# Pairing the float32 products between the projection groups of a hybrid attention and mLSTM layer

## The chip, the cores and the metric

The kernel runs on one core of a Trainium2 chip. The metric is the device time in microseconds (us) of one execution; of several executions the median is given.

## What is computed

One layer over 256 tokens of width 1024, in float32. A normalised and modulated input `h` is multiplied by a wide matrix `w_in`, and the result is cut into the inputs of two mixers. The first mixer is causal softmax attention with eight heads, the second an mLSTM with four. Both outputs are gated, normalised, projected, added and projected again:

```python
h = _rmsnorm(x, norm_w) * (1 + scale) + shift
(qa, ka, va, za, qm, km, vm, zm, om, ig, fg, ga, gm) = jnp.split(h @ w_in, SPLIT_IDX, axis=-1)
ya = merge(_moba_attention(qa, ka, heads(va, ATT_HEADS), rel_bias))
ya = (ya * jax.nn.silu(za)) @ w_att_proj
qk = jax.nn.silu(_causal_dwconv(jnp.concatenate([qm, km], axis=-1), conv_w, conv_b))
...
hm = _mlstm_chunkwise(...)
hm = jax.nn.sigmoid(heads(om, ML_HEADS)) * hm
hm = _rmsnorm(hm, ml_norm_w)
ym = (merge(hm) * jax.nn.silu(zm)) @ w_ml_proj
y = jax.nn.sigmoid(ga) * ya + jax.nn.sigmoid(gm) * ym
return x + gate * (y @ w_out)
```

With 256 tokens the attention has a single block, and the kernel computes the mLSTM in its parallel form: decayed scores times values.

## The kernel before

**Phase one** (until about 58 us) loads `x`, the modulation weights and the first columns of `w_in`, normalises, and makes `hTh` and `hTl`: the modulated input, transposed, split into a part that the type float32r holds and the rest. Nothing of it is changed.

**The projection groups.** The rest of all projections is cut into 25 chunks of 512 output columns: ka, va (two halves), za, qm, km, att, zm, vm, om, ga, gm, ml and out, each later one in two halves. A chunk has four groups, so there are 100 groups, counted by `g`; a group covers 256 rows of the contraction. For each group the weights are split into `wh` (ScalarE, L423) and `wl` (VectorE, L427, in a few groups GpSimd), and TensorE multiplies in three products: high by high, low by high, high by low. All of these are float32r. In chunks of kind `ws` (za, qm, km, att, ga, gm, ml) the weights are the stationary operand; there a group is 24 products of 256 columns (L964, L966, L967), from the loops over two `kk`, four `i` and three products. In chunks of kind `tok` (ka, va, zm, vm, om) it is 12 products of 512 columns (L957 to L959).

**The ring.** `wh` and `wl` have five buffers each. At the start of group g the program issues the split of group g + 4, so a split that is late by less than about three groups holds nobody up.

**The mixers' own work** stands between the groups. `at(step, fn, args)` puts a function into a list, and at each group g the functions of that list run before the group's products are issued. Since all engines take their instructions in the program's order, the step number sets where on each engine the function's instructions stand. A number is written as `done(name, half)`, the first group after that chunk, plus an offset. The functions that matter here multiply plain float32, not float32r:

- `att_av(h0)` (L609): probabilities times values for two heads. TensorE L617 and L619; then VectorE L623 and ScalarE L624 and GpSimd L625, which make `yah` and `yal`, the moving operand of chunk att.
- `ml_scores(h)` (L714): scores of one mLSTM head, four products at L720, two of 128 and two of 256 columns. Then VectorE L722, ScalarE L726, GpSimd L727, which make the two parts of `SD`.
- `ml_T(kp)` (L767): four 128 x 128 transposes at L775; then twice ScalarE L779 and VectorE L780, which make `ymh` and `yml`, the moving operand of chunk ml.

Beside these, `att_PT` (L601, three transposes of probabilities), `att_qk` (L574), `qk_T` (L460) and `gates_T` (L559) are plain float32 too and stay where they are. `ml_num` (L729) is float32r. Each of these functions takes a PSUM tile from a pool called `aux` with four buffers; the chunks' own tiles, called `mm`, have two.

The trace shows each plain float32 product as two matmul instructions: the four products of an `ml_scores` are a row with x8.

Of the kernel before, what the change touches and what calls it, by code (L numbers as in the profile page):

```python
# [64 lines left out]
def tile_hybrid(ctx: ExitStack, tc: tile.TileContext, x, c, params, params2, rel_t, w_row, ada_mod, ada_gate,  # L65
# [257 lines left out]
    def done(name, half):  # L323
        return 4 * (C[name, half] + 1)
# [107 lines left out]
    def at(step, fn, *a):  # L432
        hooks.setdefault(step, []).append((fn, a))
# [416 lines left out]
    for nm in ("qm", "km"):  # L850
        for hf in range(2):
            s = done(nm, hf)
# [1 line left out]
                at(s + q, lambda i, *a: conv(mmt[i], *a), C[nm, hf], hf, nm, q)  # L854
                at(s + q + 1, conv_silu, hf, nm, q)
    for q in range(2):
        at(done("za", 0) + 1 + q, att_av, 2 * q)
        at(done("za", 1) + 1 + q, att_av, 4 + 2 * q)
    s = done("km", 0)
    at(s + 3, ml_scores, 0)  # L860
    at(s + 4, ml_scores, 1)
    s = done("km", 1)
    at(s + 3, ml_scores, 2)
    at(s + 4, ml_scores, 3)
    at(4 * C["att", 0] - 10, gate_init)
    gate_left = {}
    for q, nm in enumerate(GSEG):
        s = 4 * C[nm, 0] - 4
# [7 lines left out]
    for hp in range(2):  # L876
        s = done("om", hp)
        at(s + 1, ml_num, 2 * hp)
        at(s + 2, ml_num, 2 * hp + 1)
        at(s + 3, ml_y, hp)  # L880
        at(s + 7, ml_T, 2 * hp)
        at(s + 8, ml_T, 2 * hp + 1)

    A = HB - 1
# [142 lines left out]
```

## Time and profile before

| | |
|---|---|
| median of 3 runs | 354.27 us (354.25 to 354.75) |
| profiled execution, first to last instruction | 352.7 us |
| median less that span | 1.6 us |
| TensorE busy | 348.1 us, 99% of the span |
| VectorE busy | 241.5 us, 68% |
| ScalarE busy | 210.4 us, 60% |
| GpSimd busy | 91.0 us, 26% |
| HBM traffic | 220 GB/s over the span |

TensorE's matmuls overlap in the trace: a product's row shows when it started and how long until its modelled end, and the next one has usually started before that end. How long a product holds the array is therefore read from one start to the next start, not from the duration.

### The profile page before, as it was taken

What the parts mean: (1) busy time and instruction counts of PE and PEld (TensorE: products, weight loads), DVE (VectorE), ACT (ScalarE), POOL (GpSimd) and SP (SyncE); (2) the same over time, 40 slices, a digit from 0 to 9 for tenths busy, and PEclk for the clock granted to TensorE, in tenths of its full rate; (3) what the DMA queues carried; (4) which work ended last, traced back from release to release, by engine and by line L of the source; (5) the groups of instructions that cost most, each with busy time, mean ns of one, the idle gap of its engine ahead of it and who ended that gap; (6) DMA issues with size and microseconds to landing.
All of it is one profiled execution on the core that took longest, in us unless ns stands there. A gap on an engine that the chain in (4) does not pass through costs nothing.

```text
span 352.7 us, 6115 instructions
## 1 busy us (share of the span) xinstructions
PE 348.1 (99%) x2418; PEld 322.0 (91%) x2418; DVE 241.5 (68%) x359; ACT 210.4 (60%) x327; POOL 91.0 (26%) x93
## 2 busy tenths in 40 slices
PE   8999999999999999999999999999999999999996
PEld 5987889888999999999999888888899999999996
DVE  3899998889964427767775474664475675668961
ACT  4776799987785776775555444554646375443510
POOL 4950005583005043554340000000010420534000
PEclk9999999999999999999999999999999999999999
DMA  7999999994671363494673955749309219353011
GB/s 301 418 420 420 415 380 354 215 270 202 241 254 48 109 250 121 117 397 144 220 257 122 360 216 198 298 127 373 95 9 355 115 39 372 128 215 145 2 59 61
DMA packets 24574, 77.96 MB, mean 221 GB/s; under 512 B 2909, under 2 KB 5985, under 8 KB 24034
## 3 DMA queue, kind: packets, MB, share of 16 engines
q1 hardware_dynamic: 24240, 77.03, 61.0%
q10 hardware_dynamic: 306, 0.55, 0.5%
q8 instruction: 19, 0.31, 0.3%
q14 instruction: 9, 0.07, 0.1%
HBM read 76.12 MB, written 1.45 MB: 220 GB/s over the span
## 4 chain that ended last, share of the span: by engine, by line
PE 89%; DMA 8%; ACT 1%; issue 0%; SPq 0%; DVE 0%; ACTq 0%
PE mm L964 15%; PE mm L966 14%; PE mm L967 14%; PE mm L957 9%; PE mm L959 9%; PE mm L958 9%; DMA raw<-in_w_row_dram 8%; PE pm L186 4%; PE mm L950 3%; PE aux L720 1%; PE aux L617 1%; PE mm L977 1%; PE mm L979 1%; PE mm L978 1%; PE aux L467 1%; PE aux L579 1%
## 5 line engine op out<-in xcount | busy, mean ns | idle before, releaser
L427 DVE TENSOR_TENSOR wl<-raw,wh 128x1024 fp32r<-128x1024 f32 (+1 forms) x92 | 116.0, 1273 | 66.2 <-ACT wh L423 66.2
L423 ACT CAST wh<-raw 128x1024 fp32r<-128x1024 f32 (+1 forms) x100 | 102.1, 1031 | 60.0 <-PE mm L959 31.4
L964 PE MATMUL mm<-hTh,wh 128*128 128x256 f32 x320 | 90.3, 282 | 0.0
L966 PE MATMUL mm<-hTl,wh 128*128 128x256 f32 x320 | 88.9, 278 | 0.0
L967 PE MATMUL mm<-hTh,wl 128*128 128x256 f32 x320 | 88.8, 278 | 0.0
L964 PEld LDWEIGHTS mm<-hTh,wh 128*128 128x128 f32 x320 | 60.3, 188 | 0.1
L966 PEld LDWEIGHTS mm<-hTl,wh 128*128 128x128 f32 x320 | 60.2, 188 | 0.1
L967 PEld LDWEIGHTS mm<-hTh,wl 128*128 128x128 f32 x320 | 60.2, 188 | 0.0
L957 PE MATMUL mm<-wh,hTh 128*128 128x512 f32 (+1 forms) x144 | 55.0, 382 | 0.0
L959 PE MATMUL mm<-wh,hTl 128*128 128x512 f32 (+1 forms) x144 | 54.4, 378 | 0.0
L958 PE MATMUL mm<-wl,hTh 128*128 128x512 f32 (+1 forms) x144 | 54.4, 378 | 0.0
L959 PEld LDWEIGHTS mm<-wh,hTl 128*128 128x128 f32 x144 | 27.0, 188 | 5.1
L958 PEld LDWEIGHTS mm<-wl,hTh 128*128 128x128 f32 x144 | 27.1, 188 | 4.7
L957 PEld LDWEIGHTS mm<-wh,hTh 128*128 128x128 f32 x144 | 27.1, 188 | 4.6
L427 POOL TENSOR_TENSOR wl<-raw,wh 128x1024 fp32r<-128x1024 f32 x8 | 19.6, 2463 | 18.4 <-ACT wh L423 18.4
L757 POOL TENSOR_SCALAR f<-f 128x4 f32<-128x4 f32 x2 | 0.4, 197 | 86.9 <-DVE f L756 86.9
L175 DVE TENSOR_TENSOR wrl<-raw,wrh 128x512 fp32r<-128x512 f32 (+1 forms) x24 | 18.1, 776 | 1.2 <-ACT wrh L170 0.8
L964 PE MATMUL mm<-yah,wh 128*128 128x256 f32 x64 | 18.3, 286 | 0.0
L967 PE MATMUL mm<-yah,wl 128*128 128x256 f32 x64 | 17.7, 277 | 0.0
L966 PE MATMUL mm<-yal,wh 128*128 128x256 f32 x64 | 17.7, 277 | 0.0
L170 ACT CAST wrh<-raw 128x512 fp32r<-128x512 f32 (+1 forms) x24 | 15.8, 684 | 3.3 <-DMA raw<-in_w_row_dram 3.3
L967 PE MATMUL mm<-ymh,wl 128*128 128x256 f32 x64 | 17.7, 276 | 0.0
(210 smaller groups left out, 678.0 us busy)
## 6 DMA issues: line engine op xcount, KB each, us to landing
raw<-in_w_in_dram SPq DMA_DIRECT2D x36, 1024.0 KB, 5.0
adat<-in_ada_mod_dram SPq DMA_DIRECT2D x16, 512.0 KB, 9.4
raw<-in_ada_gate_dram SPq DMA_DIRECT2D x4, 1024.0 KB, 5.7
raw<-in_w_att_proj_dram SPq DMA_DIRECT2D x4, 1024.0 KB, 7.7
raw<-in_w_ml_proj_dram SPq DMA_DIRECT2D x4, 1024.0 KB, 6.8
raw<-in_w_out_dram SPq DMA_DIRECT2D x4, 1024.0 KB, 7.3
raw<-in_w_row_dram SPq DMA_DIRECT2D x4, 896.0 KB, 12.3
raw<-in_w_row_dram SPq DMA_DIRECT2D x4, 640.0 KB
```

Source lines behind the costliest of these rows:

```text
L170: copy(wsp[k][0][:, c0:c1], wrow[k][:, c0:c1])
L175: e.tensor_tensor(l[:, cs], wrow[k][:, cs], h[:, cs].bitcast(F32), op=OP.subtract)
L186: nc.tensor.matmul(pm[ch][:, t], a[:, k, t * 128:(t + 1) * 128], b[:, cs], start=k == 0 and i == 0 and (ch < 3 or t == 0), stop=k == KT - ...
L423: nc.scalar.copy(h, w)
L427: e.tensor_tensor(l, w, h.bitcast(F32), op=OP.subtract)
L950: nc.tensor.matmul(mmt[ci][:, t, cs], a, w[:, kk, cs], start=first and i == 0 and c0 == 0 and w is wh, stop=last and i == 1 and c0 > 0, sk ...
L957: nc.tensor.matmul(o, a, wh[:, kk], start=first, stop=False)
L958: nc.tensor.matmul(o, a, wl[:, kk], start=False, stop=False)
L959: nc.tensor.matmul(o, b, wh[:, kk], start=False, stop=last)
L964: nc.tensor.matmul(o, wh[:, kk, cs], sh_[:, k], start=first and i % 2 == 0, stop=False, skip_group_check=True)
L966: nc.tensor.matmul(o, wh[:, kk, cs], sl_[:, k], start=False, stop=False, skip_group_check=True)
L967: nc.tensor.matmul(o, wl[:, kk, cs], sh_[:, k], start=False, stop=last and i % 2 == 1, skip_group_check=True)
```

## The change

Eight steps are renumbered, nothing else. The second half of a pair of functions stays where it was, and the first half moves to just ahead of it, so that the two are issued one right after the other.

```diff
     for q in range(2):
-        at(done("za", 0) + 1 + q, att_av, 2 * q)
-        at(done("za", 1) + 1 + q, att_av, 4 + 2 * q)
+        at(done("za", 0) + 2, att_av, 2 * q)
+        at(done("za", 1) + 2, att_av, 4 + 2 * q)
     s = done("km", 0)
-    at(s + 3, ml_scores, 0)
+    at(s + 4, ml_scores, 0)
     at(s + 4, ml_scores, 1)
     s = done("km", 1)
-    at(s + 3, ml_scores, 2)
+    at(s + 4, ml_scores, 2)
     at(s + 4, ml_scores, 3)
...
         at(s + 3, ml_y, hp)
-        at(s + 7, ml_T, 2 * hp)
+        at(s + 8, ml_T, 2 * hp)
         at(s + 8, ml_T, 2 * hp + 1)
```

In group numbers: `att_av` of the first two pairs of heads stood at groups 17 and 18 and now stands at 18; of the last two at 21 and 22, now 22. `ml_scores` stood at 35 and 36, now 36, and at 39 and 40, now 40. `ml_T` stood at 71 and 72, now 72, and at 75 and 76, now 76. So six places hold a double set of float32 products where twelve held a single one.

The first place is TensorE at group 36, the first of chunk att, with the scores of heads 0 and 1. Before, one head's scores stand there, between the last product of chunk km and the first of chunk att:

```order
L967 MATMUL mm<-hTh,wl 128x256
L720 MATMUL aux<-qmT,kmT 128x128 x2
L720 MATMUL aux<-qmT,kmT 128x256 x2
L964 MATMUL mm<-yah,wh 128x256
L966 MATMUL mm<-yal,wh 128x256
```

After the change both heads' scores stand there:

```order
L967 MATMUL mm<-hTh,wl 128x256
L720 MATMUL aux<-qmT,kmT 128x128 x2
L720 MATMUL aux<-qmT,kmT 128x256 x2
L720 MATMUL aux<-qmT,kmT 128x128 x2
L720 MATMUL aux<-qmT,kmT 128x256 x2
L964 MATMUL mm<-yah,wh 128x256
L966 MATMUL mm<-yal,wh 128x256
```

The other set came from 24 products earlier, from ahead of group 35. At group 40 the same happens with heads 2 and 3.

The second place is TensorE at group 76, the first of chunk gm, with the transposes of the second mixer's output. Before:

```order
L966 MATMUL mm<-hTl,wh 128x256
L967 MATMUL mm<-hTh,wl 128x256
L775 MATMUL aux<-ident,omt 128x128 x4
L964 MATMUL mm<-hTh,wh 128x256
L966 MATMUL mm<-hTl,wh 128x256
```

After:

```order
L966 MATMUL mm<-hTl,wh 128x256
L967 MATMUL mm<-hTh,wl 128x256
L775 MATMUL aux<-ident,omt 128x128 x8
L964 MATMUL mm<-hTh,wh 128x256
L966 MATMUL mm<-hTl,wh 128x256
```

Four of the eight came from ahead of group 75.

The third place is ScalarE around the groups 71 to 76, as one piece of the difference. `wh` is the split of a group four ahead, `gat` the evacuation of chunk ga, `ymh` that of the transposes:

```order
-L423 CAST wh<-raw 128x1024
-L779 ACTIVATE ymh<-aux,prm_68 128x256 x2
-L423 CAST wh<-raw 128x1024
+L423 CAST wh<-raw 128x1024 x2
 L691 ACTIVATE gat<-mm 128x1024
-L779 ACTIVATE ymh<-aux,prm_68 128x256 x2
-L423 CAST wh<-raw 128x1024 x3
-L779 ACTIVATE ymh<-aux,prm_68 128x256 x2
-L423 CAST wh<-raw 128x1024
+L779 ACTIVATE ymh<-aux,prm_68 128x256 x4
+L423 CAST wh<-raw 128x1024 x4
 L691 ACTIVATE gat<-mm 128x1024
```

The evacuations of a pair of transposes move together behind the evacuation of chunk ga, and the splits of four groups (77 to 80) stand behind them in one row. VectorE's L780 move likewise.

## The prediction

> **What bounds the kernel now.** I read the page first: the span, the engines' busy time, the granted clock, the chain that ended last.
>
> ```profile
> span 352.7 us, 6115 instructions
> PE 348.1 (99%) x2418; PEld 322.0 (91%) x2418; DVE 241.5 (68%) x359; ACT 210.4 (60%) x327; POOL 91.0 (26%) x93
> PEclk9999999999999999999999999999999999999999
> PE 89%; DMA 8%; ACT 1%; issue 0%; SPq 0%; DVE 0%; ACTq 0%
> ```
>
> TensorE (PE) is busy 99% of the span at the full clock, and the chain is 89% TensorE; its DMA share is the loading at the start. So I asked whom TensorE waited for.
>
> ```profile
> PE warm L217 <- POOL ident masks.py:199: 1.4, 1, 1.4
> ```
>
> That is its only wait, in the first microseconds. All that the change moves lies after 100 us, where TensorE goes from product to product. The time can change only through what TensorE's own products take, or through a wait that does not exist yet.
>
> A busy time of 99% does not tell how closely the products follow each other. For that I took TensorE's timeline around the scores of one head and around a set of `att_av`, and read starts against starts.
>
> ```profile
> 119.70 0.59 PE L617 MATMUL aux<-PT,vat 128*128 128x256 f32 x2
> 120.13 0.39 PE L619 MATMUL aux<-PT,vat 128*128 128x128 f32 x2
> 120.35 0.60 PE L617 MATMUL aux<-PT,vat 128*128 128x256 f32 x2
> ...
> 160.32 0.28 PE L967 MATMUL mm<-hTh,wl 128*128 128x256 f32 x1
> 160.44 1.47 PE L720 MATMUL aux<-qmT,kmT 128*128 128x128 f32 x8
> 161.56 0.47 PE L964 MATMUL mm<-hTh,wh 128*128 128x256 f32 x1
> 161.86 0.28 PE L966 MATMUL mm<-hTl,wh 128*128 128x256 f32 x1
> 161.98 0.28 PE L967 MATMUL mm<-hTh,wl 128*128 128x256 f32 x1
> ```
>
> The first float32r product after the scores seems to stall: from 161.56 to 161.86 is 0.30 us, where its neighbours take 0.12. The sum says otherwise. Two float32 instructions of 256 columns take 0.43 us (119.70 to 120.13), two of 128 columns 0.22 (120.13 to 120.35). The scores are four of each, 2 x 0.43 + 2 x 0.22 = 1.30 us, and one float32r product is 0.11 to 0.12. From 160.44 to 161.86 are 1.42 us, which is 1.30 + 0.12. The product is only recorded early, while the last score instruction still runs. I call the part of its 0.30 us that belongs to the scores the overhang: 0.30 - 0.11 = 0.19 us.
>
> So changing from float32 to float32r costs about nothing in itself. What does differ is the pace of the float32r products afterwards. I cut the trace into the stretches between one set of float32 products and the next (the columns are from:to, length, TensorE's busy time, instructions that touch the stretch, clock, DMA):
>
> ```profile
> 111.00:113.91 2.91, 2.91 (x27) 1.00 0.00 0
> 114.16:119.70 5.54, 5.54 (x51) 1.00 0.00 0
> 120.92:123.75 2.83, 2.83 (x28) 1.00 0.93 352
> 124.97:160.44 35.47, 35.47 (x316) 1.00 0.59 210
> 161.56:164.57 3.01, 3.01 (x26) 1.00 0.18 26
> 165.70:174.06 8.36, 8.36 (x74) 1.00 0.58 200
> 175.18:178.20 3.02, 3.02 (x27) 1.00 0.84 258
> 179.32:190.41 11.09, 11.09 (x99) 1.00 0.66 238
> 268.77:271.60 2.83, 2.83 (x28) 1.00 1.04 401
> 271.95:280.52 8.57, 8.57 (x75) 1.00 0.43 153
> 280.87:283.70 2.83, 2.83 (x28) 1.00 0.00 0
> 284.05:305.91 21.86, 21.86 (x195) 1.00 0.57 217
> ```
>
> By the loops a group is 24 products, so these hold 24, 48, 24, 312, 24, 72, 24, 96, 24, 72, 24 and 192. After `att_av` and the transposes the overhang is 0.09 (0.20 less 0.11, rows below). The longest stretch gives the pace: (35.47 - 0.09) / 312 = 0.1134 us. Length less count times pace less overhang is the excess, in the table's order: 0.10, 0.01, 0.02, 0, 0.10, 0.01, 0.11, 0.01, 0.02, 0.32, 0.02, 0. There are two paces, 113.4 ns a product and about 4.4 ns more (0.32 / 72; 0.10 / 24), and a stretch keeps the one that it has after its first few products. Four of twelve are slow: the ones of groups 18, 35, 39 and 72 to 74. The clock is 1.00 in both, and the DMA share is both low and high in both, so neither makes it. It also occurs without a float32 set ahead:
>
> ```profile
> 257.88 0.28 PE L964 MATMUL mm<-hTh,wh 128*128 128x256 f32 x1
> 260.71 0.28 PE L738 MATMUL aux<-vaug,SD 128*128 128x258 f32 x1
> ```
>
> These are the 24 products of group 68, (260.71 - 257.88) / 24 = 117.9 ns, after a row of 512-column products. What chooses the pace the trace doesn't tell; that a set of float32 products can flip it does stand there, both ways.
>
> **The change, part by part.** No instruction is removed or added. Six sets move down by one group, five of these leave their place free of float32 products altogether; at group 17 `att_PT` and `gates_T` remain.
>
> 1. The five stretches that no longer begin with a set. Groups 21, 35, 39, 71 and 75 now follow on from the stretch before. Their excess of 0.02 + 0.10 + 0.11 + 0.02 + 0.02 = 0.27 us goes, if the stretch before is at the fast pace. Those ahead of 21 (114.16:119.70) and 35 (124.97:160.44) were; those ahead of 39, 71 and 75 hang on point 3 and on groups 68 to 70. Bounds: a stretch that stays slow keeps its 0.10, so -0.17 and -0.27; I take -0.27.
>
> 2. The second set behind the first, without float32r products between. By the rows of `att_av` above (two L617, two L619, two L617, in 0.43 and 0.22 steps) float32 sets follow one another without a gap: 0.
>
> 3. The pace behind each double set. No row shows one. Group 18 (slow, 0.10) begins with `att_PT` and now two sets: -0.10 to 0. Groups 72 to 74 (slow, 0.32) become 72 to 75 behind eight transposes: -0.32 if fast, 96 x 4.4 - 0.32 = +0.10 if slow. For the transposes these rows show the small difference that goes with the two paces:
>
> ```profile
> 268.42 0.60 PE L775 MATMUL aux<-ident,omt 128*128 128x128 f32 x4
> 268.77 0.37 PE L964 MATMUL mm<-hTh,wh 128*128 128x256 f32 x1
> 268.98 0.28 PE L966 MATMUL mm<-hTl,wh 128*128 128x256 f32 x1
> ...
> 271.60 0.60 PE L775 MATMUL aux<-ident,omt 128*128 128x128 f32 x4
> 271.95 0.36 PE L964 MATMUL mm<-hTh,wh 128*128 128x256 f32 x1
> 272.15 0.28 PE L966 MATMUL mm<-hTl,wh 128*128 128x256 f32 x1
> ```
>
> The same four instructions ahead of a fast stretch and of a slow one, alike to 0.01 us up to the second product. Three of four such sets ended fast, but at this place it was slow; I take the middle, -0.10 for this point in all. The stretches behind groups 22, 36, 40 and 76 were fast behind a single set (0, 0.01, 0.01, 0); I keep them so, and price the other outcome as a rival. One piece more can move: group 68 to 70 lie ahead of the transposes and behind everything else; I leave them as they are.
>
> 4. The other engines. VectorE and ScalarE evacuate two sets in a row, with the splits of later groups behind them. The tightest place is group 76:
>
> ```profile
> 278.79 1.21 DVE L427 TENSOR_TENSOR wl<-raw,wh 128x1024 fp32r<-128x1024 f32 x1
> 279.92 0.47 DVE L780 SCALAR_TENSOR_TENSOR yml<-aux,prm,ymh 128x256 fp32r<-128x256 f32 x1
> 280.93 0.48 DVE L780 SCALAR_TENSOR_TENSOR yml<-aux,prm,ymh 128x256 fp32r<-128x256 f32 x1 [0.54 <-ACT ymh L779]
> 281.87 3.50 DVE L427 TENSOR_TENSOR wl<-raw,wh 128x1024 fp32r<-128x1024 f32 x3 [0.46 <-ACT wh L423]
> ...
> 284.05 0.37 PE L964 MATMUL mm<-hTh,wh 128*128 128x256 f32 x1
> ...
> 286.87 0.28 PE L964 MATMUL mm<-hTh,wh 128*128 128x256 f32 x1
> ```
>
> The L427 at 278.79 is for group 76 (TensorE at 284.05), the first of the three at 281.87 for group 77, done at about 283.1, while TensorE comes at 286.87: 3.8 us of cover. After the change the two L780 of the other transposes, 1.0 us each with their ScalarE half, stand here too, 2.0 us; but they no longer stand in front of the chain that makes `omt`, which starts about 1.3 us earlier. That takes 0.7 us of the 3.8. At groups 36 and 40 one L722 and one L726 more stand ahead of a split, about 0.5 us each, less than the 3.8. So 0, and one microsecond for each one beyond the cover. GpSimd's share (L625, L727) is wanted only several groups later.
>
> The sum against the profiled execution: -0.27 - 0.10 = -0.37, rounded -0.4: a span of 352.3. Median and span are 1.6 us apart; with that kept, 354.27 - 0.4 = 353.9 us. This case alone reaches from -0.7 (points 1 and 3 in full: 0.27 + 0.42) to -0.2: 353.6 to 354.1.
>
> **The rivals.**
>
> *A slow pace behind a double set, middle stretches.* Groups 36 to 39 or 40 to 43 become slow: 96 x 4.4 ns = 0.42 us each. For it: each first set of scores did end slow, twice of two; against it: each second one ended fast, twice of two, and the second set is what ends the pair now. Result 354.3 for one, 354.7 for both: no change.
>
> *The same, in a long stretch.* This is the case on the other side. The pair at group 22 is followed by groups 22 to 35, 336 products: 336 x 4.4 ns = +1.5 us, so 353.9 + 1.5 = 355.4. The pair at group 76 is followed by 192 products of chunk gm, +0.84 (354.7), and as many of chunk ml, together +1.7 (355.6). It undoes the forecast's gain from 0.4 / 0.0044 = 90 slow products on and is slower than the 0.2% from 250 on. For it: four slow stretches in twelve, one of 72 products that did not recover. Against: all the stretches behind these places' own second sets were fast before, over 312 and 192 products, and `att_av` alone always ended fast.
>
> *Switching does cost.* If the 0.30 us of the first product after the scores and the 0.20 after the others were a stall after all, each place given up would save 0.19 (35, 39) or 0.09 (21, 71, 75): 0.65 us more, 353.9 - 0.65 = 353.2. Against it stands the sum above.
>
> *A cover that fails, or the clock.* If the splits came over 3.8 us late, TensorE would wait; and eight transposes in a row are new here. The eight of the query rows show that such a run leaves the clock at full (all 9 in the page's row):
>
> ```profile
> 63.92 1.04 PE L467 MATMUL aux<-ident,qt 128*128 128x128 f32 x8
> ```
>
> If the clock did fall to half for as long as eight transposes take, about 0.9 us, it would cost 0.9 at each of two places: 353.9 + 1.8 = 355.7. The Trainium skill has a rule that speaks for this: by "TensorE: Matmul & The Clock Gate", Part 4, transposes do not count as work that keeps the clock up. By that rule longer runs of them are a risk; the clock in this trace does not bear it out.
>
> **How the numbers follow.** Chances: the forecast 0.50; middle stretches slow 0.17; a long stretch slow 0.17; switching costs 0.11; cover or clock 0.05. The likeliest gives 353.9. A measurement of this kernel tells some 0.2% from no change, 0.7 us, so the bounds are 353.56 and 354.98. Faster by more: the switching case, and 0.06 of the forecast's (its lower end is just there, and groups 68 to 70 might turn fast): 0.17. Slower by more: the long stretch except where it is chunk gm alone, 0.13, and the last case, 0.05: 0.18. Same: the rest, 0.65. The range goes from the switching case, 353.2, up to 355.2, which leaves out most of the long stretch and the last case: about 0.15.
>
> **What would show it.** Right: TensorE's only wait is still L217; sets of x16 at L720 and x8 at L775; groups 35 and 39 at 113.4 ns, 2.72 us without overhang; the stretches behind the pairs at the same pace; a span of 352.0 to 352.5. Wrong: 117.8 ns over a stretch of hundreds of products; TensorE idle with L427 or L423 as the releaser near group 77; a first product after a pair that, with the pair's own instructions, takes over 0.05 us more than 0.43 and 0.22 for each two and 0.11 for itself; a digit below 9 in the clock's row; or a gain above 0.7 us without a stretch that changed its pace.

## The result

The changed kernel takes 356.53 us (median, 356.51 to 357.67), the kernel before in the same session 354.30 us (354.25 to 354.75): a ratio of 1.0065, 95% interval 1.0051 to 1.0078. It is slower by 2.2 us, where 353.9 us and 353.2 to 355.2 were forecast. The spans of the two profiled executions are 354.6 and 352.7 us.

The page after, in the lines that were read of before:

```profile
span 354.6 us, 6116 instructions
PE 350.1 (99%) x2418; PEld 323.8 (91%) x2418; DVE 240.7 (68%) x359; ACT 210.4 (59%) x327; POOL 92.6 (26%) x93
PEclk9999999999999999999999999999999999999999
PE 99%; POOL 0%; DVE 0%; issue 0%; POOLq 0%
```

The same 2418 matmuls keep TensorE busy 2.0 us longer, at the same full clock, and at the same 99%. (In this execution the chain goes back along TensorE to the start; before, its first 8% went along the loading.) TensorE's waits, all of them:

```profile
PE warm L217 <- POOL ident masks.py:199: 1.4, 1, 1.4
```

So nobody made it wait. Now the stretches between the sets of float32 products, which are groups 17, 18, 19 to 21, 22 to 35, 36 to 39, 40 to 43, 72 to 75 and 76 to 83 (from:to, length, busy time, instructions, clock, DMA share and GB/s):

```profile
105.05:107.99 2.94, 2.94 (x26) 1.00 0.86 302
110.86:113.69 2.83, 2.83 (x28) 1.00 0.00 0
113.93:122.19 8.26, 8.26 (x75) 1.00 0.24 74
124.72:164.39 39.67, 39.67 (x340) 1.00 0.51 186
166.82:178.32 11.50, 11.50 (x99) 1.00 0.65 223
180.75:192.24 11.49, 11.49 (x98) 1.00 0.47 178
273.77:285.16 11.39, 11.39 (x99) 1.00 0.36 134
285.96:307.81 21.85, 21.85 (x195) 1.00 0.59 217
```

Read as in the prediction: length, less products times 0.1134, less the overhang of 0.09 or, behind scores, 0.19. Groups 22 to 35 are 336 products: 39.67 - 38.10 - 0.09 = 1.48 us of excess, 4.4 ns for each product. Groups 36 to 39 and 40 to 43 have 0.42 and 0.41, groups 72 to 75 have 0.41, group 17 has 0.11 (its overhang too is 0.11), the others within 0.02 of nothing. Added up before rounding, these are 2.85 us, against 0.71 before: 2.14 more. From the start of group 0 (58.38 us before, 58.14 after) to the end the kernel became 354.6 - 58.14 - (352.7 - 58.38) = 2.14 us longer. Next to nothing is left for any other cause.

At the turn itself, the pair of `att_av` at group 22, TensorE's timeline shows nothing:

```profile
123.28 0.38 PE L619 MATMUL aux<-PT,vat 128*128 128x128 f32 x2
123.50 0.60 PE L617 MATMUL aux<-PT,vat 128*128 128x256 f32 x2
123.93 0.38 PE L619 MATMUL aux<-PT,vat 128*128 128x128 f32 x2
...
124.72 0.37 PE L964 MATMUL mm<-hTh,wh 128*128 128x256 f32 x1
124.93 0.28 PE L966 MATMUL mm<-hTl,wh 128*128 128x256 f32 x1
```

The second set, from 123.50, follows the first in the steps of 0.22 and 0.43 us of the prediction, and the first float32r product takes 0.21, as elsewhere. The 1.5 us are not lost in the set. They are lost in 336 products behind it, 4 ns at a time.

### The profile page after: what moved, and what is told of

It reads as the page before. It is cut to its first block, busy times and chain, and to the rows that moved or that the text cites. A ratio compares the mean times of both kernels' runs of the same rounds, so it can differ in the third digit from the quotient of the medians.

```text
span 354.6 us, 6116 instructions
## 1 busy us (share of the span) xinstructions
PE 350.1 (99%) x2418; PEld 323.8 (91%) x2418; DVE 240.7 (68%) x359; ACT 210.4 (59%) x327; POOL 92.6 (26%) x93
## 4 chain that ended last, share of the span: by engine, by line
PE 99%; POOL 0%; DVE 0%; issue 0%; POOLq 0%
PE mm L964 15%; PE mm L966 15%; PE mm L967 15%; PE pm L186 9%; PE mm L957 9%; PE mm L958 9%; PE mm L959 9%; PE mm L950 3%; PE pg L186 2%; PE aux L720 1%; PE xps L243 1%; PE pc L224 1%; PE warm L217 1%; PE mm L978 1%; PE mm L979 1%; PE mm L977 1%
## 5 line engine op out<-in xcount | busy, mean ns | idle before, releaser
L964 PE MATMUL mm<-ymh,wh 128*128 128x256 f32 x64 | 17.7, 276 | 0.0
L966 PE MATMUL mm<-yml,wh 128*128 128x256 f32 x64 | 17.7, 276 | 0.0
```

Of the source, the lines that this page charges most:

```text
L964: nc.tensor.matmul(o, wh[:, kk, cs], sh_[:, k], start=first and i % 2 == 0, stop=False, skip_group_check=True)
L966: nc.tensor.matmul(o, wh[:, kk, cs], sl_[:, k], start=False, stop=False, skip_group_check=True)
```

## The experiments

The question was what sets the pace. I call the theories by letters. **P**: the set of float32 products itself, together with the pace that TensorE has when it begins; for one head's scores it turns the pace over. **D**: any double set leaves slow. **E**: the evacuations of two sets in a row (VectorE, ScalarE) disturb TensorE's reads. Later: **R**, long sets leave slow; **N**, it is chance; **A**, the paces come from where the operands lie in SBUF; **Q**, what counts is a set's content, and a product more or less repairs a place.

The kernel before itself ranged from 353.9 to 356.2 us in these sessions. In the profiled executions of all the kernels group 0 starts between 57.6 and 59.1 us, before anything that an experiment touches. So the stretches tell more than the times. Each kernel was profiled once.

**One part alone: the values.** Of the change, only the two lines of `att_av`, in the kernel before.

```diff
-        at(done("za", 0) + 1 + q, att_av, 2 * q)
-        at(done("za", 1) + 1 + q, att_av, 4 + 2 * q)
+        at(done("za", 0) + 2, att_av, 2 * q)
+        at(done("za", 1) + 2, att_av, 4 + 2 * q)
```

> Only the probabilities times values are paired (groups 18 and 22); scores and transposes stand as before. Theory P (history): what pace a set of float32 products leaves depends on the set and on the pace that stood before it; a set of scores turned fast into slow and slow into fast in the kernel before. Then groups 22 to 34 are slow as in the changed kernel (312 products, +1.37), group 35 turns fast (-0.10), 36 to 38 turn slow (+0.31), 39 fast (-0.11), 40 to 43 slow (+0.42): 356.2 us. Rival D (double): it is the double set itself that leaves the slow pace, and single sets do what they did before: +1.37 alone, 355.6 us. Rival E (evacuations): VectorE and ScalarE, busy with two sets in a row, slow TensorE; then the slow pace would end once they are through, a few us behind group 22, 354.4 us.

Measured: 355.99 us against 354.27, ratio 1.0050 (1.0035 to 1.0065). Groups 22 to 34, 35, 36 to 38, 39, and 40 to 43:

```profile
124.44:161.27 36.83, 36.83 (x315) 1.00 0.55 202
162.40:165.32 2.92, 2.92 (x26) 1.00 0.32 56
166.44:175.11 8.67, 8.67 (x74) 1.00 0.55 186
176.24:179.16 2.92, 2.92 (x26) 1.00 0.79 241
180.28:191.78 11.50, 11.50 (x99) 1.00 0.62 214
```

The excesses are 1.36, 0.01, 0.32, 0.01 and 0.42: slow, fast, slow, fast, slow. Before, the same four single sets of scores gave slow, fast, slow, fast. Each of them turned the pace over in both kernels; only what they started from is reversed. A pair of values at group 22 therefore spoiled even stretches whose own sets are untouched. Groups 22 to 34 stay slow for 312 products, long after the evacuations of the pair, so E falls.

**One part alone: the scores.**

```diff
-    at(s + 3, ml_scores, 0)
+    at(s + 4, ml_scores, 0)
...
-    at(s + 3, ml_scores, 2)
+    at(s + 4, ml_scores, 2)
```

> Only the scores are paired (groups 36 and 40). Theory P: the stretch of groups 22 to 35 is fast here, two sets of scores turn the pace twice, so 36 to 39 and 40 to 43 are fast, and the slow groups 35 and 39 of before are gone: 354.3 - 0.2 = 354.1 us. Rival D: both double sets leave the slow pace, 96 products each, +0.42 twice: 354.3 - 0.2 + 0.84 = 354.9 us. Rival E: the slow pace only for a few us behind each pair, 354.2 us.

Measured: 354.92 us, ratio 1.0016 (1.0005 to 1.0027). Groups 22 to 35, 36 to 39, 40 to 43:

```profile
124.32:162.51 38.19, 38.19 (x340) 1.00 0.54 196
164.94:176.44 11.50, 11.50 (x99) 1.00 0.74 244
178.87:190.37 11.50, 11.50 (x99) 1.00 0.55 190
```

Groups 22 to 35 are fast now (excess 0), and both pairs of scores leave slow, 0.42 each: the first from a fast start, the second from a slow one. P as I had put it, that two turns cancel, is wrong here; D has its number. A pair is not two single sets one after the other.

**One part alone: the transposes.**

```diff
-        at(s + 7, ml_T, 2 * hp)
+        at(s + 8, ml_T, 2 * hp)
```

> Only the transposes are paired (groups 72 and 76). Theory P: the pace ahead of group 72 is fast as it was in both kernels, so 72 to 75 are slow and 76 on fast, as in the changed kernel: 354.3 - 0.04 + 0.09, 354.35 us, no change. Rival D in its strict form: the double set at 76 leaves slow as well, +0.84 or more, over 355.1 us. Rival E: at most 354.5 us.

Measured: 354.73 us, ratio 1.0008 (0.9994 to 1.0023): not told from no change. Groups 72 to 75 and 76 to 83:

```profile
272.69:284.09 11.40, 11.40 (x100) 1.00 0.32 113
284.88:306.74 21.86, 21.86 (x195) 1.00 0.57 217
```

Excess 0.42 and 0. The first pair of transposes leaves slow, the second one, eight transposes like it, fast. So D is wrong as a rule too.

**One place undone.** The change without the pair at group 22: heads 4 and 5 stay at group 21.

```diff
-        at(done("za", 1) + 2, att_av, 4 + 2 * q)
+        at(done("za", 1) + 1 + q, att_av, 4 + 2 * q)
```

> The changed kernel with one of its six pairs undone: the values of the last heads stand at groups 21 and 22 again. Theory P: groups 22 to 35 are fast as before (1.48 us less than changed), and since the scores then come from the fast pace, their pairs leave it fast, 0.84 less: 356.5 - 2.3 = 354.2 us, with 72 to 75 still slow. Rival D: only the stretch of 22 to 35 recovers, 36 to 43 stay slow: 355.0 us. Rival E: most of the change's cost would stay spread over the five other pairs, 356 us.

Measured: 355.14 us against 354.27, ratio 1.0022 (1.0012 to 1.0032). Groups 22 to 35, 36 to 39 and 40 to 43:

```profile
125.01:163.19 38.18, 38.18 (x339) 1.00 0.54 196
165.62:177.12 11.50, 11.50 (x98) 1.00 0.74 245
179.56:191.05 11.49, 11.49 (x98) 1.00 0.55 189
```

38.18 in place of 39.67: this single place cost 1.49 us, two thirds of the whole loss. The pairs of scores leave slow as before.

**Sets of one to twelve transposes.** To see what a set's length does, the kernel before gets further sets, of n = 1 to 12 transposes of the identity, ahead of groups 23 to 34. Their results go nowhere; they are pure extra work, so only the stretches behind them are read.

```diff
+    def extra(n):
+        pa = aux([128, 128])
+        for _ in range(n):
+            nc.tensor.transpose(pa, ident, ident)
+
+    for n in range(1, 13):
+        at(22 + n, extra, n)
```

> The kernel before with twelve added sets ahead of groups 23 to 34: 1, 2, 3 and so on to 12 float32 transposes of the identity into an aux tile that nobody reads, so that each set is followed by 24 products of the same kind. It adds 78 transposes at 0.11, 8.6 us, 362.9 us in all. Theory Q: a set's length in instructions decides which pace it leaves, in a fixed and not monotonous way, so the twelve stretches are a mixture of 113.4 and 117.8 ns, with 8 slow as at group 72 and 3 and 4 fast. Rival R (long sets): every set over some length leaves the slow pace and every shorter one the fast one: a single step between two numbers, 8 and above slow. Rival N (chance): the stretches differ without regard to the set, and in a second kernel would come out otherwise.

Measured: 363.72 us (one run). The stretches of 24 products behind n = 3, 4, 5, and 8, 9, 10 (fast would be 2.81 to 2.85, slow 2.91 to 2.92):

```profile
133.48:136.30 2.82, 2.82 (x28) 1.00 0.88 282
136.65:139.56 2.91, 2.91 (x27) 1.00 0.11 41
140.03:142.85 2.82, 2.82 (x27) 1.00 0.50 160
...
150.73:153.64 2.91, 2.91 (x28) 1.00 0.98 387
154.54:157.38 2.84, 2.84 (x27) 1.00 0.87 349
158.39:161.22 2.83, 2.83 (x28) 1.00 0.88 339
```

Slow behind 4, 6, 7, 8 and 12, fast behind 1, 2, 3, 5, 9, 10 and 11. It is a mixture, as Q had it, but 4 came out slow where Q had it fast. Longer sets are not worse, so R falls; the DMA share is high and low in both.

Further down this kernel has the sets of the kernel before, unchanged. The four sets of scores start from a slow stretch here and leave fast, slow, fast, slow, as in the kernel with the values paired. The four sets of transposes did something new. These are groups 71, 72 to 74 and 75:

```profile
278.20:281.02 2.82, 2.82 (x27) 1.00 1.00 404
281.38:289.64 8.26, 8.26 (x76) 1.00 0.44 151
290.00:292.91 2.91, 2.91 (x27) 1.00 0.00 0
```

Fast, fast, slow, where the kernel before had fast, slow, fast (2.83, 8.57, 2.83). At group 72 the same four transposes follow the same fast stretch in both kernels and leave another pace. So a set and a start called fast or slow do not yet decide; what else does, these rows do not show.

**Sets of one to twelve products of 256 columns**, at the same places, again extra work whose results go nowhere.

```diff
...
+            nc.tensor.matmul(pa, ident, T["PT"][:, 0, 0:256], start=True, stop=True)
...
```

> As the scan of transposes, with 1 to 12 float32 products of 256 columns (identity by probabilities) in place of the transposes; their results go nowhere. 78 products at 0.43 us add 33.5 us, 387.9 us. Theory Q: again a mixture of the two paces. Rival R: a single step, all sets above it slow. By what the values and scores show (1.3 us of a single set of values left fast, 2.6 us of two slow) that step would lie between 3 and 6 products.

Measured: 388.93 us (one run). Behind n = 3, 4, 5, 8 and 12; the overhang is 0.19 here, so fast is 2.92 and slow 3.01:

```profile
135.36:138.29 2.93, 2.93 (x26) 1.00 0.59 239
139.83:142.84 3.01, 3.01 (x26) 1.00 0.30 73
144.81:147.75 2.94, 2.94 (x26) 1.00 0.00 0
...
162.11:165.12 3.01, 3.01 (x26) 1.00 0.96 295
...
191.30:194.31 3.01, 3.01 (x26) 1.00 0.00 0
```

Slow behind 4, 8 and 12, fast behind all nine others. R falls here too: a set of eleven is harmless, a set of four is not. That the length makes this period of four is not shown. The three slow sets stand at groups 26, 30 and 34, the third group of a chunk each time, and behind these three groups the transposes left slow too. The lengths were run in one order only, so length and place are not told apart. Against N, chance, speaks what repeats: in this kernel, too, the four sets of scores start slow and leave fast, slow, fast, slow. The four single sets turned the pace over each time in all five kernels that have them, twice from a fast start and three times from a slow one.

**The weights at another address.** The split weights `wh` and `wl` of a `ws` chunk lie 80 elements into their ring slot. Three kernels put them at 0, 64 and 96, in the changed kernel.

```diff
-RING, WS_AT = 1152, 80
+RING, WS_AT = 1152, 0
```

> The changed kernel with the weight tiles of kind ws at offset 0 of their ring buffers in place of 80 elements; nothing else. Theory A (addresses): the two paces come from how the weight load's reads fall against the moving operand's reads in the on-chip memory, so that another distance between their addresses gives other paces, from group 12 on, where the code is the same as in both kernels: the fast pace of 113.4 ns itself changes, or slow and fast stretches are others; 1 ns per product on 1100 products is 1.1 us. Rival T (time only): only the moments count, every stretch keeps its pace, 356.5 us.

> The changed kernel with the weight tiles of kind ws at offset 64 in place of 80 elements. At offset 0 every stretch took 120.0 ns a product. Theory A (addresses): at 64 the paces are others again than 113.4 and 117.8, or the slow one is all that is left; somewhere between 354 and 362 us. Rival: 0 was a special case, and every stretch keeps its pace of the changed kernel, 356.5 us.

> The changed kernel with the weight tiles of kind ws at offset 96 in place of 80 elements. Theory A (addresses): other paces than at 80, as for offset 64, in 354 to 362 us; if the fast pace holds everywhere, about 354 us. Rival: the paces of the changed kernel, 356.5 us.

Measured: 361.74 us for 0 (ratio 1.0209, 1.0192 to 1.0226), and in one run each 362.02 us for 64 and 360.79 us for 96. Groups 22 to 35 of the three kernels, in this order:

```profile
125.52:165.92 40.40, 40.40 (x340) 1.00 0.49 183
```

```profile
125.88:166.27 40.39, 40.39 (x339) 1.00 0.51 184
```

```profile
125.74:165.69 39.95, 39.95 (x340) 1.00 0.50 186
```

That is (40.40 - 0.09) / 336 = 120.0 ns a product for 0 and 64, and 118.6 for 96. The same products in the same order, with only the weights moved, have other paces, and of the four offsets only 80 shows 113.4 at all. At 96 there are two paces too: groups 36 to 39, where the moving operand is `yah` in place of `hTh`, took 11.70 us, which is (11.70 - 0.19) / 96 = 119.9 ns. So T falls, and A is right in that the weights' address sets the paces. That it does so by where the weights lie against the moving operand is not shown, since no run moved that operand alone.

**The same scores in another order.** The kernel with one place undone, and in each head's scores the two products of 256 columns first, the two of 128 behind them.

```diff
-        for c0, s0 in ((256, 128), (0, 0)):
+        for c0, s0 in ((0, 0), (256, 128)):
```

> The changed kernel with the values at groups 21 and 22 again, and with the scores' four products in the other order: the two of 256 columns first, the two of 128 columns last, as in the values. Theory Q: what the set ends with matters, so groups 36 to 43 need not stay slow behind the pairs: if fast, 355.1 - 0.84 = 354.3 us. Rival D (double): two sets in a row leave slow whatever their order, 355.1 us.

Measured: 354.38 us against 354.22, ratio 1.0001 (0.9992 to 1.0011). Groups 36 to 39 and 40 to 43, and the rows at the first of the two:

```profile
164.93:175.91 10.98, 10.98 (x99) 1.00 0.75 249
178.45:189.42 10.97, 10.97 (x99) 1.00 0.58 212
```

```profile
162.40 2.78 PE L720 MATMUL aux<-qmT,kmT 128*128 128x256 f32 x16
164.93 0.37 PE L964 MATMUL mm<-yah,wh 128*128 128x256 f32 x1
165.14 0.28 PE L966 MATMUL mm<-yal,wh 128*128 128x256 f32 x1
```

10.98 - 10.89 - 0.09 = 0 (the last products are of 128 columns now, so the overhang is the small one). Both pairs of scores leave fast. The pairing, the work and the evacuations are the same as where 0.42 was lost twice; only the order inside the set differs. That is the strongest of the runs against D and E.

**Transposes by two.** On top of this, each `ml_T` in halves of two transposes at four groups, since a set of two was harmless in the scan.

```diff
...
-        at(s + 8, ml_T, 2 * hp)
-        at(s + 8, ml_T, 2 * hp + 1)
+        for q in range(4):
+            at(s + 7 + q, ml_T, 2 * hp + q // 2, (q % 2,))
```

> The kernel with turned and paired scores and the values at 21 and 22, and with the transposes of the second mixer's output issued two at a time, ahead of groups 71 to 74 and 75 to 78, in place of eight at 72 and 76. In the scan two transposes left the fast pace from a fast start. Theory Q: all stretches from 71 on are fast, 0.4 us less than with the pairs, and about 0.4 us less than the kernel before: 353.9 us, near what a measurement can tell. Rival D (only pairs do harm): the same time within 0.1 us. Rival: eight boundaries in place of four each leave their own pace and some are slow, 24 products each at 0.1 us: up to 354.5 us.

Measured: 355.86 us against 354.30, ratio 1.0052 (1.0036 to 1.0069). The first three groups that begin with two transposes, 71 to 73, and then groups 78 to 83 behind the last such set:

```profile
268.08:270.93 2.85, 2.85 (x28) 1.00 1.02 397
271.06:273.98 2.92, 2.92 (x28) 1.00 0.87 285
274.11:276.96 2.85, 2.85 (x27) 1.00 0.53 216
...
289.10:306.14 17.04, 17.04 (x147) 1.00 0.61 230
```

Fast, slow, fast; over the eight sets it is fast, slow, fast, fast, slow, fast, fast, slow: every third of eight like sets leaves slow, which speaks against chance too. The last slow one is followed by 17.04 us for 144 products, (17.04 - 0.09) / 144 = 117.7 ns, and the pace stays so to the end of chunk ml, 336 products in all: the 1.5 us that this kernel takes over the one before it. The expectation was missed: a set that was harmless in the scan is not harmless here.

**One or two more products at each place.** The changed kernel with transposes of the identity behind its pairs: one at groups 22, 36 and 72, two at 40 and 76. Their results go nowhere.

```diff
...
+    for g, n in ((22, 1), (36, 1), (40, 2), (72, 1), (76, 2)):
+        at(g, extra, n)
```

> The changed kernel with seven added transposes of the identity behind its pairs: one each behind those of groups 22, 36 and 72, two each behind those of 40 and 76; their results go nowhere. They add 7 x 0.11 = 0.8 us of work. Theory Q (remainder): which pace follows hangs on how many float32 instructions the set holds, in a short period, so one or two more take a slow place out of the slow remainder: groups 22 to 35, 36 to 39, 40 to 43 and 72 to 75 turn fast, -1.48 - 0.42 - 0.42 - 0.41, and 76 on stays fast: 356.5 - 2.7 + 0.8 = 354.6 us, if all four turn. Rival D (double sets leave slow, whatever their length): 356.5 + 0.8 = 357.3 us.

Measured: 357.16 us, ratio 1.0082 (1.0067 to 1.0096). Groups 22 to 35, 36 to 39 and 40 to 43:

```profile
124.65:164.30 39.65, 39.65 (x339) 1.00 0.51 187
166.95:177.96 11.01, 11.01 (x99) 1.00 0.68 225
180.71:192.10 11.39, 11.39 (x99) 1.00 0.53 188
```

One product more made groups 36 to 39 fast (11.01 in place of 11.50). At the other places it did not: 22 to 35, 40 to 43 and 72 to 75 stayed slow, 76 stayed fast. That a set's content matters is shown once more, at groups 36 to 39; my rule for how much to add is wrong.

**What is shown, and what is open.** Shown: the loss is the slow pace of the float32r products behind four of the six pairs, and undoing one pair takes its share back to 0.01 us. The pace hangs on the content and the order of the set ahead and on the weights' address; for single sets of scores it also hangs on the pace at their start. It holds from a few products behind the set until other products come in between. No run shows it to hang on waits (TensorE has none at these places), evacuations, the clock (1.00 throughout) or DMA. Open: what in TensorE or in its reads makes the paces, and a rule that says beforehand which set leaves which. The start is more than "fast" or "slow": four transposes from a fast start left slow at group 72 of the kernel before, fast at its group 76, and fast at group 72 in the scan of transposes. None of these kernels was measurably faster than the kernel before.

## Why the prediction was wrong

- **What bounds the kernel** (TensorE's products, no wait): right. So was the reading of the two paces and of the overhang, with which every stretch at offset 80 comes out to 0.04 us.
- **Step 1**, five stretches give up 0.27: the condition stated there, that the stretch before is fast, held at 21 and 71 (0.04 in all). Groups 35, 39 and 75 joined stretches that had become slow and cost 0.10 each, as any slow group of 24 products.
- **Step 2**, the second set without a gap: right, by the rows at group 22.
- **Step 3 is the one that failed**, in the sentence "The stretches behind groups 22, 36, 40 and 76 were fast behind a single set (0, 0.01, 0.01, 0); I keep them so". Three of the four turned slow: +1.48, +0.42, +0.41. Groups 72 to 75 went to the slow bound (+0.10 on before), group 18 became fast as hoped, and group 17, with only `att_PT` and `gates_T` left ahead of it, became slow in its place. The fault was to take over a pace from behind a *single* set. The profile of before had the counterevidence: groups 35 and 36 begin with sets of the same kind and size, and one left slow, the other fast. The change altered both the set and what stood before it. Both matter; why just these three places turned slow and group 76 did not stays open.
- **The bounds**: "-0.7 to -0.2" leaves out a term of the prediction's own. With point 1 at -0.17 and groups 72 to 75 at +0.10 the upper end is -0.07, or 354.2 us.
- **Step 4**, the other engines: right. TensorE never waits at groups 76 and 77, and eight transposes in a row left the clock at 1.00.
- **The rivals**: the prices were right (0.42 for each middle stretch, 1.5 for groups 22 to 35; measured 0.42, 0.41, 1.48). They were weighed as alternatives, one or the other, and came together, because they share one cause. By their own prices all three give 353.9 + 1.5 + 0.8 = 356.2; with 72 to 75 slow rather than between the bounds, 356.4, against 356.53 measured. With a mechanism known to turn stretches either way and an unknown rule, each of four stretches deserved something like the observed four in twelve, independently, and the range an upper end to hold two of them. "Switching does cost" is refuted.

## What to carry to other kernels

When one engine is the bound and shows 99% busy, divide start to start by the number of products, stretch by stretch: two kernels with the same busy share and the same one wait at the start differed by 2.1 us in just this. A few small products between long streams can change the pace of the whole stretch up to the next set, so weigh such a set by the length of the stretch behind it (336 products here, 1.5 us), look at each stretch again after any reordering, and try the cheap handles, the order inside the set and the offset of the weights. Rivals that have the same cause belong together in a range: price them jointly.

## What the runs showed of the hardware

- A stream of weight load and float32r product of 256 columns has several steady paces at the granted clock of 1.00: 113.4 and 117.8 ns at offset 80, 120.0 at 0 and 64, 118.6 and 119.9 at 96. A stretch kept the slow one for as long as 336 products. The Trainium skill, "TensorE: Matmul & The Clock Gate", Part 2, "Back-to-back issue gap", gives one figure for an isolated product of 256 columns, 262 cycles or N/2.4 + 2.5, which comes to 109 ns, and says of a stream with weight loads that both operations set the spacing. The second is in line with the runs in which only the weights' address moved; the one figure is below all the paces measured here.
- The placement of the weights within their slot is worth over twice what the change is: offset 0 in place of 80 costs 361.74 - 356.53 = 5.2 us with the same instructions.
- A short set of float32 products can turn the pace behind it either way, and the order inside it counts: with the products of 256 columns first, the pairs of scores left 113.4 ns behind them in place of 117.8.
